# A post-norm whose factor g moves into the copy out of PSUM, and whose norm is applied on VectorE or Pool

## The chip, the cores and the metric

One core of one Trainium2 chip (trn2). Its engines are TensorE (PE in the profile), VectorE (DVE), ScalarE (ACT), Pool (GpSimd) and the DMA queues, issued by SyncE (SP). Each engine executes its own instructions in program order. The metric is the device time of one execution in microseconds.

## The reference, cut to what matters

Two layers of a streaming encoder on 1024 prompt frames and 32 sample frames, width 1024, in fp32:

```
h  = rmsnorm(x, g_pre[l])
P  = h @ w_in[l]                        # one projection, cut into three mixers
ya = gMLP(...);  yb, yc = attention of two kinds, each times silu of its gate
y  = concat(ya, yb, yc) @ w_out[l]
x  = x + rmsnorm(y, g_post[l])          # the post-norm
rmsnorm(v, g) = v * rsqrt(mean(v*v) + 1e-6) * g
```

## The kernel before

The frames lie along the free axis, in three tiles: tiles 0 and 1 of 384 columns and tile 2 of 288 (the last 32 are the sample frames). The model width lies on the partitions in eight chunks of 128. An fp32 product is taken as three products of rounded parts: the activation is split into hh and hl, the weight into whi and wlo (in rows of the profile some weights stand in buffers named kk, ph, pl or vv), and TensorE adds hh·whi, hl·whi and hh·wlo in PSUM. One block of output rows for one tile is 24 matmuls, in a PSUM tile named d or S.

A layer computes its projection blocks in the order of `ORDERS[l]`, each for all three tiles, the attention units between them, and then the eight output blocks, first all of tile 0, then of tile 1, then of tile 2. Each output block is squared for the post-norm's sum and copied out of PSUM into `Y` by ScalarE or VectorE (`copy`). Then comes `boundary(l, t)`. Ones-matmuls sum the squares over partitions, VectorE and Pool form the factor r, ident-matmuls spread it over the partitions (`rms_steps`), and ScalarE writes it to `R`. For each of the eight chunks, `x` multiplies `Y` by g and R, adds the residual chunk (buffers named s or bias) and stores the result; `x2` splits the new `Y` into hh (times the next layer's g) and hl, and adds its square, which ScalarE has written to a tmp, into a sum v. When all eight are in, the ones-matmul on v starts the norm of the next layer. The last tile of layer 1 goes through `finish` instead, where g is already applied in the copy.

The order of instructions on each engine is set when the program is built. A planner (class `Clock`) carries a modelled time for every engine and buffer; steps wait in lanes, and `look` and `pump` emit the step that the model has ready first, so that matmuls of the next blocks stand between a sum and its ones-matmul. Two helpers choose an engine by the earlier modelled end: `copy` between ScalarE and VectorE, and `two` between VectorE and Pool:

```
ends = [(clock.end(e.key, "tensor_tensor", [out], [a, b]) - bias * i, i)
        for i, e in enumerate((dve, pool))]
(dve, pool)[min(ends)[1]].tensor_tensor(out, a, b, op)
```

All engine calls pass through one recording helper, so every row of the profile carries its line, L291. Instructions are told apart by their tiles.

Of the kernel before, what the change touches and what calls it, by code (L numbers as in the profile page):

```python
# [21 lines left out]
ALU = mybir.AluOpType  # L22
# [15 lines left out]
BLOCKS = "bk bv bq0 bq1 bq2 bq3 av0 av1 ck0 ck1 cv0 cv1 cq0 cq1 au0 au1 az0 az1 bz0 bz1 bz2 bz3 cz0 cz1".split()  # L38

ORDERS = (  # L40
    "bk bv bq0 bq2 bq1 bq3 av1 cq0 cv0 ck0 av0 bz2 cq1 cv1 au0 ck1 bz1 au1 az0 az1 bz3 bz0 cz1 cz0".split(),
    "bk bv bq0 bq1 bq2 av0 ck1 cv0 bq3 bz2 bz0 av1 ck0 cq0 cq1 bz1 cv1 au1 au0 bz3 az0 az1 cz0 cz1".split(),
)

FIRST = {"b": 0, "c": 4, "a": 6}
# [261 lines left out]
def encoder(  # L307
# [87 lines left out]
    def tmp():  # L395
        return tl([128, 384], "tmp")
# [676 lines left out]

    def layer_consts(l):

        box = {}

        def mix():
            dma.dma_start(wt, aws[l])

            for g in range(4):
                pool.affine_select(wt[:, g, :], wt[:, g, :], pattern=[[1, 128]], compare_op=ALU.is_ge, fill=0.0,
                                   base=0, channel_multiplier=-1)

        def mix_bias(g):
            half = g % 2
            dma.dma_start(bsb[64 * half : 64 * half + 64, g // 2, :], abias[l, g : g + 1, :].to_broadcast([64, 128]))

        def sample_sink(j, g):
            dma.dma_start(ssk[32 * g : 32 * g + 32, j : j + 1],  # L1090
                          sinks[l : l + 1, 4 * j + g : 4 * j + g + 1].to_broadcast([32, 1]))
            if (j, g) == (1, 3):
                pool.tensor_scalar(ssk[:, 2:4], ssk[:, 0:2], -1.0, None, op0=ALU.mult)

        def table():
            c, e = box["c"], box["e"] = tmp(), tmp()
            dma.dma_start(c[:4, 0:256], crel[l, :, 1:257])
            pool.tensor_copy(c[:4, 256:384], c[:4, 255:256].to_broadcast([4, 128]))
            pool.tensor_copy(e[:4, :], c[:4, 255:256].to_broadcast([4, 384]))
            lane("store").put(lambda: dma.dma_start(fc_d[l][:, 0:384], c[:4, :]), None, lambda: after("dma", [c[:4, :]]))  # L1100
            lane("store").put(lambda: dma.dma_start(fc_d[l][:, 384:FC_W], e[:4, : FC_W - 384]), None,
                              lambda: after("dma", [e[:4, :]]), f"{l}.LC")

        return ([table, mix, lambda: dma.dma_start(gab, ag[l : l + 1, :].to_broadcast([128, 256]))]
                + [lambda g=g: mix_bias(g) for g in range(4)] + [lambda j=j, g=g: sample_sink(j, g) for j in (0, 1) for g in range(4)])

# [160 lines left out]
    def boundary(l, t, box):  # L1267

        a, T = TOK[t]
        last = l == L - 1  # L1270
        ln = lane(f"bnd{t}")
        chunk = chunks[l, t]
        rms_steps(ln, box, t, None, f"{l}.P{t}")
        nb = {}
        for k in range(8):
            y = Y[:, k, a : a + T]

            def x(k=k, y=y):
                g = g_sb[:, l, 1, k : k + 1]
                dve.scalar_tensor_tensor(y, y, g, R[:, a : a + T], op0=ALU.mult, op1=ALU.mult)  # L1280
                c = chunk.pop(k)
                two(y, y, c[:, :T], ALU.add)
                let_go(c)
                store((o_y if last else x1_d[l])[:, k, a : a + T], y)

            def x2(k=k, y=y):
                if k == 0:
                    nb["sq"] = sq_tile(t)
                h_split(l + 1, t, k)
                sq_add(nb["sq"], y, T, k == 0)  # L1290

            ln.put(x, lambda k=k: k in chunk, lambda k=k: after("dve", [R[:, a : a + T], chunk[k][:, :T]]), eng=("dve",))
            if not last:
                ln.put(x2, lambda k=k: k or free("v"), lambda y=y: after("act", [y]), f"{l + 1}.X{t}.{k}", eng=("act", "dve"))
        if not last:
            rms_steps(ln, nb, t, None, f"{l + 1}.R{t}")

    def layer_steps(l):
        units = [Unit(l, br, i, q) for br, n in (("b", 4), ("c", 2)) for i in range(n) for q in range(8 // NQ[br])]
        over = marks("0.R0") if l == 0 else marks(*(f"{l - 1}.{x}" for x in ("b3", "c1", "A", "SB", "SC")))  # L1300
        lane("lc").put(lambda: sink_consts(l), over, None, f"{l}.LS")
        for f in layer_consts(l):
            lane("lc").put(f, marks(f"{l}.b1.bias"), lambda: clock.t["dma"])
        lane("lc").put(lambda: None, None, None, f"{l}.LD")
        for i, (br, pair) in enumerate([("b", i) for i in range(4)] + [("c", i) for i in range(2)]):
            lane("bias").put(lambda br=br, pair=pair: load_bias(l, br, pair),
                             lambda br=br: f"{l}.LS" in done and (br == "b" or f"{l}.LC" in done) and "t5" in done and (l == 0 or f"{l - 1}.xl2.7" in done) and free("bias", 1 if br == "b" else 2),
                             lambda br=br: slot("bias", "dma", 1 if br == "b" else 2), f"{l}.{br}{pair}.bias")
            if (br, pair) == ("b", 1):
                sample_b_steps(l)  # L1310
        for u in units:
            u.steps()
        a_steps(l)
        sample_c_steps(l)
# [5 lines left out]
    for e, (x, t) in enumerate(plan):  # L1320
# [38 lines left out]
        if kind == "w":  # L1359
            need = [f"{l}.R{t}"]  # L1360
            if n[1] == "z" and n[0] != "a":
                need += [f"{l}.{n[0]}{n[2]}"] + ([f"{l}.S{n[0].upper()}"] if t == 2 else [])
            if n[:2] in ("au", "az"):
                need.append(f"{l}.A")

            def leave(l=l, n=n, t=t, d=d, a=a, T=T):
                evac(l, n, t, d)
                let_go(d)
                if n == ORDERS[l][-1]:
                    for k in range(KB):  # L1370
                        y = Y[:, k, a : a + T]

                        def ys(y=y, k=k):
                            split(hh[t][:, k, :], hl[t][:, k, :], y)

                        lane("ysplit").put(ys, None, lambda y=y, k=k: after("act", [y], [hh[t][:, k, :]]), f"{l}.ys{t}.{k}",
                                           eng=("act", "dve"))

            ok = marks(*need)
            lane("evac").put(leave, lambda ok=ok: ok() and free("v"), None, f"{l}.{n}.{t}")  # L1380
        else:
            if plan[e - 1][1] != t or plan[e - 1][0][0] == "w":
# [122 lines left out]
```

## Time and profile before

| what | value |
|---|---|
| device time, three runs | 1014.22, 1014.42, 1015.70 us; median 1014.42 |
| profiled execution | 1014.88 us, of which the span is 1013.2 us and 1.68 us lie around it |
| granted clock of TensorE, mean | 0.998 of 2.4 GHz |
| busy: TensorE, VectorE, ScalarE, Pool | 996.8, 762.9, 511.6, 69.5 us |
| HBM traffic | 76 GB/s over the span |

All times in the rows below are in microseconds from the start of the span, which lasts to 1013.2. The hand-over from layer 0 to layer 1 lies at about 445 to 545, the end of layer 1 from about 940 on.

### The profile page before, as it was taken

The page shows a single profiled execution, that of the slowest core. Times are in us where ns is not written, and L with a number is a line of the kernel's source. Part 1 is how long each engine was busy: PE and PEld are TensorE (multiplying, and loading weights), DVE is VectorE, ACT ScalarE, POOL GpSimd, SP SyncE. Part 2 cuts the span into 40 slices and gives each one's busy share as a digit, 9 for nine tenths or more (in the row PEclk, how much of TensorE's full clock was granted, in tenths as well). Part 3 has the DMA queues.
Part 4 walks back from the last instruction along what each step waited for, and adds up shares of the span by engine and source line. Part 5 has one row for each costly group of instructions (what it writes and reads, how often), then busy time and mean ns, then how long its engine had stood idle before and what let it go on. Part 6 is the DMA issues. An engine that isn't in the chain of part 4 may idle for free.

```text
span 1013.2 us, 18902 instructions
## 1 busy us (share of the span) xinstructions
PE 996.8 (98%) x6630; PEld 969.2 (96%) x6630; DVE 762.9 (75%) x1973; ACT 511.6 (50%) x1304; POOL 69.5 (7%) x150
## 2 busy tenths in 40 slices
PE   8999999999999999999999999999999999999997
PEld 7999999989999999999999999999899999999996
DVE  8778778877777775858897789877687787577654
ACT  7555566554444443745643566645454444356332
POOL 0100000001100000000111000000200000000121
PEclk9999999999999999999999999999999999999999
DMA  8232313212123011446543322231122212126633
GB/s 267 68 79 79 84 50 88 64 48 57 58 66 96 22 43 63 145 126 187 153 137 114 79 66 78 59 85 35 52 67 64 65 43 75 42 76 196 188 109 128
DMA packets 83343, 91.26 MB, mean 90 GB/s; under 512 B 13232, under 2 KB 59696, under 8 KB 83248
## 3 DMA queue, kind: packets, MB, share of 16 engines
q1 hardware_dynamic: 83248, 90.05, 30.2%
q8 instruction: 52, 0.85, 0.4%
q14 instruction: 43, 0.35, 0.1%
HBM read 66.11 MB, written 11.31 MB: 76 GB/s over the span
## 4 chain that ended last, share of the span: by engine, by line
PE 82%; DVE 8%; DMA 3%; ACT 3%; issue 2%; SPq 1%; POOL 1%; DVEq 0%; ACTq 0%; POOLq 0%
PE d L291 54%; PE S L291 14%; PE pt L291 8%; PE pv L291 6%; DVE Y L291 3%; DVE s L291 1%; ACT tmp L291 1%; DVE wlo L291 1%; DVE pl L291 1%; DVE v L291 1%; SPq L291 1%; DMA wraw<-in_wo_dram 1%; DVE hl L291 1%; DMA wraw<-in_w_dram 1%; DMA bias<-fb_d 1%
## 5 line engine op out<-in xcount | busy, mean ns | idle before, releaser
L291 PE MATMUL d<-hh,whi 128*128 128x384 f32 (+1 forms) x1144 | 378.6, 331 | 0.0
L291 PE MATMUL d<-hh,wlo 128*128 128x384 f32 (+1 forms) x1144 | 369.7, 323 | 0.5 <-DVE wlo L291 0.4
L291 PE MATMUL d<-hl,whi 128*128 128x384 f32 (+1 forms) x1144 | 369.0, 323 | 0.0
L291 PEld LDWEIGHTS d<-hh,whi 128*128 128x128 f32 x1144 | 215.5, 188 | 2.2 <-issue 1.7
L291 PEld LDWEIGHTS d<-hh,wlo 128*128 128x128 f32 x1144 | 215.0, 188 | 1.3 <-DVE wlo L291 1.1
L291 PEld LDWEIGHTS d<-hl,whi 128*128 128x128 f32 x1144 | 215.7, 189 | 0.3
L291 ACT ACTIVATE s<-s,nm 128x256 f32<-128x256 f32 (+5 forms) x196 | 108.5, 554 | 150.0 <-DVE nm L291 149.8
L291 DVE TENSOR_TENSOR pl<-pt,ph 128x512 fp32r<-128x512 f32 (+2 forms) x136 | 80.6, 623 | 26.2 <-ACT ph L291 25.9
L291 DVE TENSOR_TENSOR wlo<-wraw,whi 128x512 fp32r<-128x512 f32 x116 | 80.2, 693 | 14.3 <-ACT whi L291 11.0
L291 ACT ACTIVATE ph<-pt 128x512 fp32r<-128x512 f32 (+2 forms) x136 | 69.0, 542 | 25.8 <-PE pt L291 24.7
L291 DVE TENSOR_TENSOR Y<-pv,tmp 64x256 f32<-64x256 f32 x96 | 40.4, 421 | 44.2 <-ACT tmp L291 43.2
L291 PE MATMUL pv<-pl,vv 128*128 128x256 f32 (+1 forms) x288 | 71.1, 286 | 0.6 <-DVE pl L291 0.3
L291 PE MATMUL pv<-ph,vv 128*128 128x256 f32 (+1 forms) x288 | 70.0, 269 | 0.2 <-ACT ph L291 0.2
L291 PE MATMUL pt<-ident,s 128*128 128x128 f32 x488 | 68.6, 274 | 0.0
L291 ACT ACTIVATE whi<-wraw 128x512 fp32r<-128x512 f32 x94 | 58.7, 624 | 18.5 <-DMA wraw<-in_wo_dram 13.7
L291 PE MATMUL S<-kk,qh 128*128 128x256 f32 (+3 forms) x224 | 66.1, 313 | 1.2 <-DVE nm L291 1.2
L291 PE MATMUL S<-kk,ql 128*128 128x256 f32 (+3 forms) x224 | 62.1, 295 | 0.0
L291 ACT ACTIVATE tmp<-tmp 128x384 f32<-128x384 f32 (+1 forms) x48 | 23.8, 496 | 68.1 <-DVE tmp L291 68.1
L291 PEld LDWEIGHTS pt<-ident,s 128*128 128x128 f32 x488 | 56.0, 140 | 2.2 <-DVE s L291 0.5
L291 PEld LDWEIGHTS pv<-pl,vv 128*128 128x128 f32 x288 | 54.4, 189 | 3.1 <-DVE pl L291 2.4
L291 DVE CUSTOM_DVE_ANT_0 s<-S,bias,nsink 128x256 f32<-128x256 f32 (+1 forms) x128 | 54.3, 463 | 2.8 <-POOL bias L291 1.5
L291 ACT ACTIVATE tmp<-pv 64x256 f32<-64x256 f32 x96 | 36.4, 379 | 39.2 <-DVE Y L291 20.4
(183 smaller groups left out, 1765.8 us busy)
## 6 DMA issues: line engine op xcount, KB each, us to landing
wraw<-in_w_dram SPq DMA_DIRECT2D x96, 256.0 KB, 2.9
wraw<-in_wo_dram SPq DMA_DIRECT2D x72, 256.0 KB, 3.0
qr<-Y SPq DMA_DIRECT2D x384, 32.0 KB, 1.9
x_d<-Y SPq DMA_DIRECT2D x16, 192.0 KB, 3.2
out_y_dram<-Y SPq DMA_DIRECT2D x16, 192.0 KB, 2.8
Y<-in_xT_dram SPq DMA_DIRECT2D x5, 576.0 KB, 4.8
bias<-fc_d SPq DMA_DIRECT2D x8, 320.0 KB, 3.8
bias<-fb_d SPq DMA_DIRECT2D x16, 128.0 KB, 3.1
```

The costliest lines, as they stand in the source:

```text
L291: return f(*args, **kw)
```

## The change

The copy out of PSUM now multiplies every output block by its g, for all tiles of both layers. `boundary` then multiplies `Y` by `R` alone, through `two`, which takes VectorE or Pool. Two block orders change by some places, and the bias table of a layer is built in two v buffers where it was built in two tmp buffers, with its store and release by the helpers that the other stores use.

```
--- before.py
+++ after.py
@@ -38,8 +38,8 @@
 BLOCKS = "bk bv bq0 bq1 bq2 bq3 av0 av1 ck0 ck1 cv0 cv1 cq0 cq1 au0 au1 az0 az1 bz0 bz1 bz2 bz3 cz0 cz1".split()
 
 ORDERS = (
-    "bk bv bq0 bq2 bq1 bq3 av1 cq0 cv0 ck0 av0 bz2 cq1 cv1 au0 ck1 bz1 au1 az0 az1 bz3 bz0 cz1 cz0".split(),
-    "bk bv bq0 bq1 bq2 av0 ck1 cv0 bq3 bz2 bz0 av1 ck0 cq0 cq1 bz1 cv1 au1 au0 bz3 az0 az1 cz0 cz1".split(),
+    "bk bv bq0 bq2 bq1 bq3 av1 cq0 cv0 ck0 av0 bz2 cq1 cv1 au0 ck1 bz1 bz0 au1 az1 bz3 az0 cz1 cz0".split(),
+    "bk bv bq0 bq1 bq2 av0 cv0 ck1 bq3 bz2 bz0 av1 ck0 cq0 cq1 bz1 cv1 au1 au0 bz3 az0 az1 cz0 cz1".split(),
 )
 
 FIRST = {"b": 0, "c": 4, "a": 6}
@@ -1073,7 +1073,6 @@
 
     def layer_consts(l):
 
-        box = {}
 
         def mix():
             dma.dma_start(wt, aws[l])
@@ -1093,13 +1092,14 @@
                 pool.tensor_scalar(ssk[:, 2:4], ssk[:, 0:2], -1.0, None, op0=ALU.mult)
 
         def table():
-            c, e = box["c"], box["e"] = tmp(), tmp()
+            c, e = tl([128, 384], "v"), tl([128, 384], "v")
             dma.dma_start(c[:4, 0:256], crel[l, :, 1:257])
             pool.tensor_copy(c[:4, 256:384], c[:4, 255:256].to_broadcast([4, 128]))
             pool.tensor_copy(e[:4, :], c[:4, 255:256].to_broadcast([4, 384]))
-            lane("store").put(lambda: dma.dma_start(fc_d[l][:, 0:384], c[:4, :]), None, lambda: after("dma", [c[:4, :]]))
-            lane("store").put(lambda: dma.dma_start(fc_d[l][:, 384:FC_W], e[:4, : FC_W - 384]), None,
-                              lambda: after("dma", [e[:4, :]]), f"{l}.LC")
+            store(fc_d[l][:, 0:384], c[:4, :], c)
+            store(fc_d[l][:, 384:FC_W], e[:4, : FC_W - 384], e)
+            lane("store").put(lambda: None, None, None, f"{l}.LC")
+            let_go(c, e)
 
         return ([table, mix, lambda: dma.dma_start(gab, ag[l : l + 1, :].to_broadcast([128, 256]))]
                 + [lambda g=g: mix_bias(g) for g in range(4)] + [lambda j=j, g=g: sample_sink(j, g) for j in (0, 1) for g in range(4)])
@@ -1277,7 +1277,7 @@
 
             def x(k=k, y=y):
                 g = g_sb[:, l, 1, k : k + 1]
-                dve.scalar_tensor_tensor(y, y, g, R[:, a : a + T], op0=ALU.mult, op1=ALU.mult)
+                two(y, y, R[:, a : a + T], ALU.mult)
                 c = chunk.pop(k)
                 two(y, y, c[:, :T], ALU.add)
                 let_go(c)
@@ -1299,8 +1299,8 @@
         units = [Unit(l, br, i, q) for br, n in (("b", 4), ("c", 2)) for i in range(n) for q in range(8 // NQ[br])]
         over = marks("0.R0") if l == 0 else marks(*(f"{l - 1}.{x}" for x in ("b3", "c1", "A", "SB", "SC")))
         lane("lc").put(lambda: sink_consts(l), over, None, f"{l}.LS")
-        for f in layer_consts(l):
-            lane("lc").put(f, marks(f"{l}.b1.bias"), lambda: clock.t["dma"])
+        for i, f in enumerate(layer_consts(l)):
+            lane("lc").put(f, lambda i=i: f"{l}.b1.bias" in done and (i or free("v", 2)), lambda: clock.t["dma"])
         lane("lc").put(lambda: None, None, None, f"{l}.LD")
         for i, (br, pair) in enumerate([("b", i) for i in range(4)] + [("c", i) for i in range(2)]):
             lane("bias").put(lambda br=br, pair=pair: load_bias(l, br, pair),
@@ -1392,7 +1392,7 @@
                 act.activation(box["more"][:, :T], d[:, :T], AF.Square)
             else:
                 sq_add(box["sq"], d[:, :T], T, cnt == 0)
-            copy(Y[:, n, a : a + T], d[:, :T], g_sb[:, l, 1, n : n + 1] if end else None)
+            copy(Y[:, n, a : a + T], d[:, :T], g_sb[:, l, 1, n : n + 1])
             let_go(d)
             cnt += 1
             if end and cnt == KB - 1:
```

The planner then places everything anew. In what follows, names carry a buffer's number. On Pool, in the hand-over of layer 0's tile 0, from the operation that raises its r to the power (r_5798) to that of the next two; lines with a - are of before, those with a + of the change; s and bias are residual chunks:

```order
 L291 TENSOR_TENSOR r_5798<-r_5798,mhalf 128x3
-L291 TENSOR_TENSOR v_5818<-v_5818,tmp_5910 128x384
-L291 TENSOR_TENSOR r_6168<-r_6168,mhalf 128x3
-L291 TENSOR_TENSOR r_6181<-r_6181,mhalf 128x3
+L291 TENSOR_TENSOR Y<-Y,R 128x384
+L291 TENSOR_TENSOR Y<-Y,s_5465 128x384
+L291 TENSOR_TENSOR Y<-Y,R 128x384 x4
+L291 TENSOR_TENSOR Y<-Y,bias_5473 128x384
+L291 TENSOR_TENSOR Y<-Y,R 128x384 x2
+L291 TENSOR_TENSOR Y<-Y,bias_5477 128x384
+L291 TENSOR_TENSOR r_6105<-r_6105,mhalf 128x3
+L291 TENSOR_TENSOR r_6180<-r_6180,mhalf 128x3
```

Seven multiplies and three residual adds now stand on Pool where one sum v stood.

On TensorE, where the ones-matmul reads v_5840, the sum of squares of layer 1's input for tile 0 (v_5818 is the sum for layer 0's tile 1; d and S are output blocks of tiles 1 and 2). Before:

```order
L291 MATMUL S_6151<-hh_70,vv_5871 128x288
L291 MATMUL pt_6164<-ones,v_5818 128x1 x3
L291 MATMUL S_6151<-hh_70,vv_5871 128x288
L291 MATMUL S_6151<-hl_73,vv_5871 128x288
L291 MATMUL S_6151<-hh_70,vv_5871 128x288 x2
L291 MATMUL S_6151<-hl_73,vv_5871 128x288
L291 MATMUL S_6151<-hh_70,vv_5871 128x288
L291 MATMUL pt_6177<-ones,v_5840 128x1 x3
```

With the change:

```order
L291 MATMUL d_6087<-hh_69,vv_5875 128x384
L291 MATMUL d_6087<-hl_72,vv_5875 128x384
L291 MATMUL d_6087<-hh_69,vv_5875 128x384 x2
L291 MATMUL d_6087<-hl_72,vv_5875 128x384
L291 MATMUL d_6087<-hh_69,vv_5875 128x384 x2
L291 MATMUL d_6087<-hl_72,vv_5875 128x384
L291 MATMUL d_6087<-hh_69,vv_5875 128x384
L291 MATMUL pt_6101<-ones,v_5840 128x1 x3
L291 MATMUL d_6087<-hh_69,vv_5875 128x384
```

The ones-matmul on v_5840 has moved ahead of the one on v_5818, from behind 18 of the 24 matmuls of tile 2's first block to behind 9 of 24 matmuls of tile 1's fifth. Between it and the ident-matmul on r_5798 stood 168 matmuls of 128x384 and 18 of 128x288; now 129 of 128x384 stand there.

On TensorE, where the next hand-over ends. v_6195 is the sum for layer 0's tile 2 in both; the sum of layer 1's input for tile 1 is v_6220 before and v_6229 now; d_6497 is the last output block, d_6535, d_6543 and S_6604 are blocks of layer 1. Before:

```order
L291 MATMUL d_6535<-hh_68,wlo_6504 128x384
L291 MATMUL pt_6569<-ones,v_6195 128x1 x3
L291 MATMUL d_6535<-hh_68,whi_6503 128x384
L291 MATMUL d_6535<-hl_71,whi_6503 128x384
L291 MATMUL d_6535<-hh_68,wlo_6504 128x384
L291 MATMUL d_6535<-hh_68,whi_6503 128x384
L291 MATMUL d_6535<-hl_71,whi_6503 128x384
L291 MATMUL d_6535<-hh_68,wlo_6504 128x384
L291 MATMUL d_6535<-hh_68,whi_6503 128x384
L291 MATMUL d_6535<-hl_71,whi_6503 128x384
L291 MATMUL d_6535<-hh_68,wlo_6504 128x384
L291 MATMUL pt_6595<-ones,v_6220 128x1 x3
```

With the change:

```order
L291 MATMUL d_6497<-hh_70,wlo_6440 128x288
L291 MATMUL d_6543<-hh_68,whi_6469 128x384
L291 MATMUL d_6543<-hl_71,whi_6469 128x384
L291 MATMUL d_6543<-hh_68,wlo_6470 128x384
L291 MATMUL pt_6551<-ones,v_6229 128x1 x3
L291 MATMUL d_6543<-hh_68,whi_6469 128x384
L291 MATMUL d_6543<-hl_71,whi_6469 128x384
L291 MATMUL d_6543<-hh_68,wlo_6470 128x384
L291 MATMUL pt_6565<-ones,v_6195 128x1 x3
```

The ones-matmul for tile 1's sum now stands three matmuls into layer 1's first block and ahead of the one on v_6195; before it stood behind that block's 24, and behind the other.

## Rows read from the trace of the kernel before

**Rows 1.** The page: busy time of each engine over the span with the number of instructions, then the chain that ended last.

```profile
PE 996.8 (98%) x6630; PEld 969.2 (96%) x6630; DVE 762.9 (75%) x1973; ACT 511.6 (50%) x1304; POOL 69.5 (7%) x150
...
PE 82%; DVE 8%; DMA 3%; ACT 3%; issue 2%; SPq 1%; POOL 1%; DVEq 0%; ACTq 0%; POOLq 0%
```

**Rows 2.** Busy time of each engine in three stretches of the hand-over from layer 0 to layer 1, one for each tile (stretch, its length, then busy time and number of instructions of PE, PEld, DVE, ACT and POOL, the granted clock of TensorE, the share and GB/s of the DMA engines).

```profile
449.50:480.90 31.40, 31.40 (x188) 31.40 (x187) 26.77 (x48) 18.76 (x41) 1.01 (x1) 1.00 0.57 176
484.00:510.00 26.00, 25.76 (x190) 25.43 (x190) 24.09 (x42) 18.09 (x41) 4.34 (x4) 1.00 0.59 174
514.00:540.00 26.00, 25.05 (x154) 24.54 (x154) 22.09 (x56) 10.15 (x29) 3.02 (x12) 1.00 0.40 125
```

**Rows 3.** The timeline of TensorE around the hand-over of tiles 0 and 1: start, duration (us), engine, line, operation, tiles, size, how many in a row.

```profile
467.71 0.34 PE L291 MATMUL d<-hh,ph 128*128 128x384 f32 x1
...
469.80 0.34 PE L291 MATMUL d<-hh,vv 128*128 128x384 f32 x1
...
473.95 0.34 PE L291 MATMUL S<-hh,vv 128*128 128x384 f32 x1
...
481.18 0.72 PE L291 MATMUL pt<-ones,v 128*128 128x1 f32 x6
...
482.63 0.83 PE L291 MATMUL pt<-ident,r 128*128 128x128 f32 x6
483.21 0.38 PE L291 MATMUL d<-hh,vv 128*128 128x288 f32 x1
```

**Rows 4.** The timeline of VectorE from the first norm on (same columns, with idle time before it and what ended it).

```profile
449.56 0.62 DVE L291 SCALAR_TENSOR_TENSOR Y<-Y,g_sb,R 128x384 f32<-128x384 f32 x1 [3.23 <-ACT R L291]
...
456.50 0.61 DVE L291 SCALAR_TENSOR_TENSOR hl<-Y,g_sb,hh 128x384 fp32r<-128x384 f32 x1
457.03 0.55 DVE L291 TENSOR_TENSOR v<-v,tmp 128x384 f32<-128x384 f32 x1
457.50 0.61 DVE L291 SCALAR_TENSOR_TENSOR Y<-Y,g_sb,R 128x384 f32<-128x384 f32 x1
...
459.43 0.68 DVE L291 TENSOR_TENSOR vv<-wraw,vv 128x512 fp32r<-128x512 f32 x1
460.03 0.68 DVE L291 TENSOR_TENSOR pl<-wraw,ph 128x512 fp32r<-128x512 f32 x1
...
484.02 0.62 DVE L291 SCALAR_TENSOR_TENSOR Y<-Y,g_sb,R 128x384 f32<-128x384 f32 x1 [1.93 <-ACT R L291]
```

**Rows 5.** TensorE's timeline at the waits of the hand-over's end, with the matmuls that give the pitches, and the late one near the end.

```profile
505.84 0.30 PE L291 MATMUL d<-hh,wlo 128*128 128x288 f32 x1
...
506.37 0.34 PE L291 MATMUL d<-hh,whi 128*128 128x384 f32 x1
...
509.42 0.83 PE L291 MATMUL pt<-ones,v 128*128 128x1 f32 x6 [0.24 <-POOL v L291]
...
512.73 0.80 PE L291 MATMUL pt<-ones,v 128*128 128x1 f32 x6 [0.79 <-DVE r L291]
...
536.29 0.55 PE L291 MATMUL pt<-ident,v 128*128 128x128 f32 x3 [0.91 <-DVE v L291]
536.60 0.42 PE L291 MATMUL d<-hh,ph 128*128 128x384 f32 x1
...
990.99 0.41 PE L291 MATMUL S<-hh,wlo 128*128 128x288 f32 x1 [0.80 <-DVE wlo L291]
```

**Rows 6.** The timeline where Pool and VectorE work side by side: in each pair the operation of Pool and the one of VectorE beside it.

```profile
458.07 1.01 POOL L291 TENSOR_TENSOR v<-v,tmp 128x384 f32<-128x384 f32 x1 [10.78 <-ACT tmp L291]
458.14 1.36 DVE L291 TENSOR_TENSOR Y<-Y,s 128x384 f32<-128x384 f32 x1
...
501.00 1.03 POOL L291 TENSOR_TENSOR v<-v,tmp 128x288 f32<-128x288 f32 x1 [1.33 <-ACT tmp L291]
501.29 1.17 DVE L291 SCALAR_TENSOR_TENSOR Y<-Y,g_sb,R 128x384 f32<-128x384 f32 x1
...
984.12 0.81 POOL L291 TENSOR_TENSOR v<-v,tmp 128x288 f32<-128x288 f32 x1 [0.30 <-ACT tmp L291]
984.15 1.19 DVE L291 SCALAR_TENSOR_TENSOR Y<-Y,g_sb,R 128x384 f32<-128x384 f32 x1
```

**Rows 7.** Groups of instructions over the whole span, different shapes apart: line, engine, operation, tiles, size, how many | busy us, mean ns | idle before.

```profile
L291 DVE SCALAR_TENSOR_TENSOR Y<-Y,g_sb,R 128x384 f32<-128x384 f32 x32 | 23.6, 739 | 11.5 <-ACT R L291 11.5
...
L291 ACT ACTIVATE Y<-d,g_sb 128x288 f32<-128x288 f32 x5 | 2.5, 496 | 0.0
...
L291 ACT ACTIVATE Y<-d 128x288 f32<-128x288 f32 x5 | 2.0, 404 | 0.0
```

**Rows 8.** VectorE's timeline in the hand-over of tile 2.

```profile
520.07 0.51 DVE L291 SCALAR_TENSOR_TENSOR hl<-Y,g_sb,hh 128x288 fp32r<-128x288 f32 x1
520.50 0.45 DVE L291 TENSOR_TENSOR v<-v,tmp 128x288 f32<-128x288 f32 x1
520.86 0.51 DVE L291 SCALAR_TENSOR_TENSOR Y<-Y,g_sb,R 128x288 f32<-128x288 f32 x1
```

**Rows 9.** Busy time and granted clock (PEclk) in three stretches of the start (columns as in rows 2).

```profile
10.00:12.00 2.00, 1.15 (x6) 0.52 (x4) 1.90 (x5) 2.00 (x5) 0.00 (x0) 1.00 0.73 260
12.00:14.00 2.00, 1.64 (x6) 1.65 (x7) 2.00 (x5) 2.00 (x5) 0.00 (x0) 0.66 0.98 301
14.00:16.00 2.00, 2.00 (x8) 2.00 (x7) 2.00 (x4) 1.87 (x5) 0.00 (x0) 0.50 0.83 252
```

More of the change, by code (lines that the diff above doesn't have):

```diff
@@ L40 @@
 ORDERS = (
-    "bk bv bq0 bq2 bq1 bq3 av1 cq0 cv0 ck0 av0 bz2 cq1 cv1 au0 ck1 bz1 au1 az0 az1 bz3 bz0 cz1 cz0".split(),
-    "bk bv bq0 bq1 bq2 av0 ck1 cv0 bq3 bz2 bz0 av1 ck0 cq0 cq1 bz1 cv1 au1 au0 bz3 az0 az1 cz0 cz1".split(),
+    "bk bv bq0 bq2 bq1 bq3 av1 cq0 cv0 ck0 av0 bz2 cq1 cv1 au0 ck1 bz1 bz0 au1 az1 bz3 az0 cz1 cz0".split(),
+    "bk bv bq0 bq1 bq2 av0 cv0 ck1 bq3 bz2 bz0 av1 ck0 cq0 cq1 bz1 cv1 au1 au0 bz3 az0 az1 cz0 cz1".split(),
 )
@@ L1074, in layer_consts @@
     def layer_consts(l):
-        box = {}
         def mix():
@@ L1095, in table @@
         def table():
-            c, e = box["c"], box["e"] = tmp(), tmp()
+            c, e = tl([128, 384], "v"), tl([128, 384], "v")
             dma.dma_start(c[:4, 0:256], crel[l, :, 1:257])
@@ L1099, in table @@
             pool.tensor_copy(e[:4, :], c[:4, 255:256].to_broadcast([4, 384]))
-            lane("store").put(lambda: dma.dma_start(fc_d[l][:, 0:384], c[:4, :]), None, lambda: after("dma", [c[:4, :]]))
-            lane("store").put(lambda: dma.dma_start(fc_d[l][:, 384:FC_W], e[:4, : FC_W - 384]), None,
-                              lambda: after("dma", [e[:4, :]]), f"{l}.LC")
+            store(fc_d[l][:, 0:384], c[:4, :], c)
+            store(fc_d[l][:, 384:FC_W], e[:4, : FC_W - 384], e)
+            lane("store").put(lambda: None, None, None, f"{l}.LC")
+            let_go(c, e)
         return ([table, mix, lambda: dma.dma_start(gab, ag[l : l + 1, :].to_broadcast([128, 256]))]
@@ L1279, in x @@
                 g = g_sb[:, l, 1, k : k + 1]
-                dve.scalar_tensor_tensor(y, y, g, R[:, a : a + T], op0=ALU.mult, op1=ALU.mult)
+                two(y, y, R[:, a : a + T], ALU.mult)
                 c = chunk.pop(k)
@@ L1301, in layer_steps @@
         lane("lc").put(lambda: sink_consts(l), over, None, f"{l}.LS")
-        for f in layer_consts(l):
-            lane("lc").put(f, marks(f"{l}.b1.bias"), lambda: clock.t["dma"])
+        for i, f in enumerate(layer_consts(l)):
+            lane("lc").put(f, lambda i=i: f"{l}.b1.bias" in done and (i or free("v", 2)), lambda: clock.t["dma"])
         lane("lc").put(lambda: None, None, None, f"{l}.LD")
@@ L1394, in encoder @@
                 sq_add(box["sq"], d[:, :T], T, cnt == 0)
-            copy(Y[:, n, a : a + T], d[:, :T], g_sb[:, l, 1, n : n + 1] if end else None)
+            copy(Y[:, n, a : a + T], d[:, :T], g_sb[:, l, 1, n : n + 1])
             let_go(d)
```

## The prediction

> **What bounds the kernel now.** I read the page first, for the engine that never rests. TensorE is busy 98% of the span and carries 82% of the chain that ended last [rows 1], so the time moves only where TensorE stands still or runs at its lower clock. VectorE is busy 75%, but that is a mean. In the stretches where layer 0 hands over to layer 1 it is nearly full: 26.77 of 31.40 us for tile 0, 24.09 of 26.00 for tile 1, 22.09 of 26.00 for tile 2 [rows 2]. There lies the change: `boundary` multiplies, adds the residual, splits into hh and hl and sums squares, and a ones-matmul on TensorE waits for the last sum.
>
> TensorE executes in program order, so the place of that ones-matmul decides who waits. For tile 0 the norm reaches VectorE at 449.56 [rows 4], and TensorE takes the sum at 481.18 with no idle time shown before it [rows 3]. At the end of the next hand-over two ones-matmuls came 0.24 and 0.79 us late, and a later ident-matmul 0.91 [rows 5]: 1.94 us, most of what TensorE loses in this part.
>
> **What one multiply costs where.** The fused multiply Y·g·R takes 0.61 us when alone and has a pitch of 0.64 (457.50 to 458.14) [rows 4, 6]; hl has one of 0.53, an add or a sum 0.47, a 128x512 subtraction 0.60 [rows 4]; for tile 2, 0.43 for hl and 0.36 for a sum [rows 8]. Pool's two-operand operation of 128x384 takes 1.01 us, of 128x288 0.81 [rows 6]. What matters more: while Pool runs one, a VectorE operation that reads two operands from SBUF is held. The 128x384 add at 458.14 took 1.36 beside Pool, and a sum of that size 0.55 alone; fused multiplies took 1.17 and 1.19 beside Pool's 128x288, against 0.61 [rows 4, 6]. So a Pool operation costs a full VectorE about 0.8 us (128x384) or 0.6 (128x288): more than the 0.47 of a plain multiply on VectorE itself.
>
> The Trainium skill (GPSIMD Engine Reference, Specifications) says that Pool's SBUF interfaces are shared with VectorE, with contention for VectorE instructions that have two SBUF inputs. These rows agree; by that rule no multiply sent to Pool is free while VectorE has such work.
>
> **The change part by part.**
>
> Copies out of PSUM: ScalarE's copy with g takes 496 ns against 404 without (128x288) [rows 7], 0.09 more each, on an engine busy 18.76 of 31.40 us [rows 2]. Zero; ScalarE's idle time hides it. Uncovered it would be 0.09 us for each of eight copies of a tile, 0.7.
>
> Removed: 40 fused multiplies on VectorE, 32 of them of 128x384 [rows 7]. By the order, 13 come back there as a plain multiply and 27 go to Pool: 7, 5 and 5 for the tiles of layer 0, 5 and 5 in layer 1. Residual adds and sums move too: in the three hand-overs Pool now executes 10, 9 and 9 operations, where before it had 1, 4 and none.
>
> Moved: TensorE asks for the sums sooner. I count operations in the order and take matmul pitches of 0.174 us for 128x384 (12 from 467.71 to 469.80) and 0.1325 for 128x288 (four from 505.84 to 506.37) [rows 3, 5].
>
> Tile 0: the ident-matmul that starts it stands in the same row in both programs. The ones-matmul of 481.18 now stands 15 matmuls ahead of the S block that began at 473.95: 473.95 - 15 × 0.174 = 471.3. From 449.56 VectorE has 21.8 us, not 31.6. Ahead of the last sum its order has 35 operations: 17 multiplies, adds and sums (17 × 0.47 = 8.0), 10 hl and hh (10 × 0.53 = 5.3), 8 of 128x512 (4.8): 18.1 us. Pool's 10 hold it for 10 × 0.8 = 8.0. I take 0.2 for the signal to TensorE, an estimate near the 0.24 of rows 5. 26.3 - 21.8 = **4.5 us** of new wait. From below: if all of Pool's work falls into VectorE's idle time, 18.3, no wait. From above: 4.6 us of the old stretch were idle on VectorE [rows 2]; 3 of them coming back would give 7.5. I stay with the sum, since idle time both lengthens VectorE's stretch and gives Pool free room.
>
> Tile 1: from ident-matmul 482.63 to the next matmul 0.58, to the first multiply 1.39 [rows 3, 4]. Then 165 matmuls of 128x288 and 3 of 128x384: 0.58 + 21.9 + 0.5 - 1.39 = 21.6 us. VectorE's 38 operations: 16 × 0.47 + 4 × 0.37 + 9 × 0.53 + 9 × 0.60 = 19.2. Pool: 7 × 0.8 + 2 × 0.6 = 6.8. 26.2 - 21.6 = **4.6 us**; bounds 0 and 6.
>
> Tile 2: 108 matmuls of 128x384 (18.8), 8 score matmuls at no more than a 128x288 (1.1), two ident groups at 0.31 (0.6) [rows 5], 0.58 - 1.39: 19.7 us. VectorE: 9 × 0.43, 14 × 0.37, and 14 operations of layer 1's keys, values and queries at about a sum's 0.47: 15.7. Pool 9 × 0.6 = 5.4. 21.3 - 19.7 = **1.6 us**; bounds 0 and 3.
>
> Layer 1's boundaries ask for no sum of squares. What waits there is one matmul at 990.99, 0.80 behind VectorE's wlo, just after Pool and VectorE held each other around 984.12 [rows 5, 6]. Five multiplies gone to Pool: 5 × (0.8 - 0.64); three that stay save 0.17 each: +0.3. I take **+0.5**, bounds -0.8 and +1.5.
>
> Gained back: 0.24, 0.79 and 0.91 [rows 5]. The first two end in the earlier places; ahead of the third, VectorE's order now has the value that TensorE needs before the scores that stood in its way: **-1.9**.
>
> At nothing: the block orders (the same matmuls, TensorE has others beside them) and the bias table in v buffers, written well before its use. If that cover went, the price is a wait as at 536.29, 0.9 us [rows 5].
>
> Sum: 4.5 + 4.6 + 1.6 + 0.5 - 1.9 = +9.3. The profiled execution took 1014.88 (span 1013.2 and 1.68 around it), 0.46 over the median of 1014.42; so 1024.2 in its terms, **1023.7** beside the median.
>
> **The rivals.**
>
> Faster: the multiplies fit. Pool is busy 7% [rows 1], and VectorE has idle time in each stretch. If Pool's work falls there, the new waits are zero, -1.9 stays and 990.99 gives back 0.8: 1014.42 - 2.7 = 1011.7. It decides if Pool's ten operations hold VectorE under 0.35 us each (21.8 - 0.2 - 18.1 = 3.5). Against: each hold of rows 6 is 0.56 or more. For: the one Pool sum in the old first stretch cost TensorE nothing. 19%.
>
> About the same: holds of 0.5 us. Then the waits are 1.5, 2.3 and 0.7; less 1.9 and up to 1 elsewhere: +1.6, 1016.0. For: the old stretch with four Pool sums lost TensorE about 1.0 us at its two ones-matmuls [rows 5]. 13%.
>
> Slower, with the clock on top. In 10 to 12 us TensorE was busy 1.15 of 2 us, and then its granted clock was 0.66 and 0.50 of 2.4 GHz, the lower level of 1.2 GHz in the last [rows 9]: 2 × 0.34 + 2 × 0.50 = 1.7 us lost. Two long waits could each cost that: 1023.7 + 3.4 = 1027.1. 8%. The Trainium skill (TensorE: Matmul & The Clock Gate, HAM oscillation) has idle gaps of TensorE taking the clock back to its lower level; the start of this trace agrees, and whether waits like these bring it about in the middle no row tells.
>
> **How the numbers follow.** My forecast, waits at the first two hand-overs and a small third, 60%. With holds of 0.56, the smallest, and no wait at tile 2 or in layer 1: 2.1 + 2.8 - 1.9 = +3.0, 1017; with the upper ends, 7.5 + 6 + 1.6 + 1.5 - 1.9 = +14.7, 1029. That is its own range. For 8 in 10 I take 1011 to 1030: down to the faster rival and up past the clock's, leaving out the clock on top of the longest waits. A measurement of this kernel tells about 0.2%, 2 us, from no change: faster 0.19, same 0.13, slower 0.68.
>
> **What would show it.** Idle time of some 4 us on TensorE before the ones-matmul for tile 0 near 471, and as much before that for tile 1, ended by VectorE's v; Pool's Y<-Y,R at 1.0 us or more, with adds and hl of VectorE at 1.1 to 1.4 beside them; VectorE near 100% busy there. If there is no gap near 471, or VectorE keeps 0.55 beside Pool, the step of the holds is wrong, and the time is 1011 to 1013. If the gap is there and the total is not, TensorE got back elsewhere what I count as fixed.

## The result

The changed kernel takes 1030.32 us (median of 4 runs, 1029.22 to 1031.04) against 1015.06 for the kernel before, timed beside it: a ratio of 1.0142 with a 95% interval of 1.0129 to 1.0156, slower by about 14.4 us (the medians lie 15.3 apart). The profiled execution took 1030.6 us, its span 1028.9, which is 15.7 more than before.

### The profile page after: what moved, and what is told of

Its sections match the earlier page's. It is cut to its first block, busy times and chain, and to the rows that moved or that the text cites. A ratio compares the mean times of both kernels' runs of the same rounds, so it can differ in the third digit from the quotient of the medians.

```text
span 1028.9 us, 18896 instructions
## 1 busy us (share of the span) xinstructions
PE 1001.5 (97%) x6630; PEld 972.5 (95%) x6630; DVE 763.8 (74%) x1935; ACT 513.1 (50%) x1304; POOL 113.2 (11%) x188
## 4 chain that ended last, share of the span: by engine, by line
PE 77%; DVE 12%; ACT 3%; issue 3%; DMA 3%; SPq 2%; POOL 0%; DVEq 0%; ACTq 0%; POOLq 0%
PE d L291 51%; PE S L291 13%; PE pt L291 8%; PE pv L291 6%; DVE Y L291 3%; SPq L291 2%; DVE v L291 2%; DVE s L291 1%; ACT tmp L291 1%; DVE pl L291 1%; DVE hl L291 1%; DVE wlo L291 1%; DMA wraw<-in_wo_dram 1%; ACT s L291 1%; DMA bias<-fb_d 1%
## 5 line engine op out<-in xcount | busy, mean ns | idle before, releaser
L291 ACT ACTIVATE ph<-pt 128x512 fp32r<-128x512 f32 (+2 forms) x136 | 68.8, 540 | 26.6 <-PE pt L291 25.8
L291 ACT ACTIVATE whi<-wraw 128x512 fp32r<-128x512 f32 x91 | 56.6, 624 | 13.5 <-DMA wraw<-in_wo_dram 8.4
L291 DVE TENSOR_TENSOR v<-v,tmp 128x384 f32<-128x384 f32 (+1 forms) x76 | 44.0, 582 | 25.5 <-ACT tmp L291 24.3
```

Of the source, the lines that this page charges most:

```text
L291: return f(*args, **kw)
```

## The profile after

The page of the changed kernel, busy times and the chain that ended last; they answer to [rows 1]:

```profile
PE 1001.5 (97%) x6630; PEld 972.5 (95%) x6630; DVE 763.8 (74%) x1935; ACT 513.1 (50%) x1304; POOL 113.2 (11%) x188
...
PE 77%; DVE 12%; ACT 3%; issue 3%; DMA 3%; SPq 2%; POOL 0%; DVEq 0%; ACTq 0%; POOLq 0%
```

VectorE lost 38 operations and is no less busy: what it saved came back as longer operations beside Pool. Its share of the chain grew from 8 to 12%. TensorE's waits in the hand-over, from its timeline; they answer to [rows 3, 5]:

```profile
475.13 0.80 PE L291 MATMUL pt<-ones,v 128*128 128x1 f32 x6 [3.95 <-DVE v L291]
...
512.76 0.40 PE L291 MATMUL d<-hh,wlo 128*128 128x288 f32 x1 [1.60 <-DVE wlo L291]
...
516.89 1.16 PE L291 MATMUL pt<-ones,v 128*128 128x1 f32 x6 [1.99 <-DVE v L291]
...
546.11 0.33 PE L291 MATMUL S<-kk,ql 128*128 128x128 f32 x1 [1.56 <-DVE ql L291]
...
553.63 0.85 PE L291 MATMUL pt<-ident,r 128*128 128x128 f32 x6 [0.94 <-POOL r L291]
```

Those are tile 0 (3.95), tile 1 (1.60 and 1.99) and tile 2 (1.56 and 0.94), 10.0 us; the waits of 0.24, 0.79 and 0.91 in [rows 5] are gone. VectorE's timeline in tile 0's stretch, and a row of Pool's beside it; they answer to [rows 4, 6]:

```profile
449.81 1.25 DVE L291 TENSOR_TENSOR Y<-Y,s 128x384 f32<-128x384 f32 x1
451.17 0.98 DVE L291 TENSOR_SCALAR hh<-Y,g_sb 128x384 fp32r<-128x384 f32 x1
452.19 1.26 DVE L291 SCALAR_TENSOR_TENSOR hl<-Y,g_sb,hh 128x384 fp32r<-128x384 f32 x1
...
455.76 1.37 DVE L291 TENSOR_TENSOR v<-v,tmp 128x384 f32<-128x384 f32 x1
...
463.10 0.61 DVE L291 SCALAR_TENSOR_TENSOR hl<-Y,g_sb,hh 128x384 fp32r<-128x384 f32 x1
463.63 0.54 DVE L291 TENSOR_TENSOR v<-v,tmp 128x384 f32<-128x384 f32 x1
...
451.90 4.82 POOL L291 TENSOR_TENSOR Y<-Y,R 128x384 f32<-128x384 f32 x4
```

And the same stretch in two windows, with Pool busy and without (columns as in [rows 2]):

```profile
449.30:462.10 12.80, 12.80 (x75) 12.80 (x74) 12.59 (x11) 6.19 (x13) 12.49 (x10) 1.00 0.31 93
463.10:475.00 11.90, 8.09 (x47) 7.76 (x45) 11.90 (x25) 10.51 (x22) 0.00 (x0) 1.00 0.79 240
```

While Pool executes its ten operations, VectorE gets through 12 in 13.9 us (449.22 to 463.10), about one to each of Pool's; then 25 in 11.9. Both windows show VectorE full, so it has no idle time into which Pool could fall. Last, the clock. The same view for two longer stretches and a piece of each; the granted clock is the third figure from the end:

```profile
470.00:486.00 16.00, 12.05 (x67) 11.76 (x66) 7.09 (x15) 7.25 (x16) 0.86 (x1) 0.89 0.50 163
500.00:530.00 30.00, 26.14 (x159) 25.39 (x158) 23.54 (x41) 15.70 (x34) 8.31 (x9) 0.89 0.61 184
...
476.00:478.00 2.00, 2.00 (x8) 2.00 (x8) 0.13 (x2) 0.00 (x0) 0.86 (x1) 0.55 0.99 344
...
518.00:520.00 2.00, 2.00 (x10) 2.00 (x9) 0.85 (x2) 0.98 (x2) 0.86 (x1) 0.50 0.87 288
```

After the waits at tile 0 and at tile 1 the clock granted to TensorE fell to 0.50 of 2.4 GHz, its lower level of 1.2 GHz. In the waits themselves it was still 1.00 (471 to 475 and 513 to 517), so the loss falls on work. Full-speed work lost: 16 × 0.11 = 1.8 and 30 × 0.11 = 3.3 us, 5.1 in all. After the waits at tile 2 it stayed at 1.00.

So the 15.7 us are: waits of 10.3 (the five above and one of 0.27 at 507.70) less the old 1.9, 8.4; the clock 5.1; and a remainder of 2.2, lost in layer 1's attention between about 555 and 605 us, where the planner placed things differently and no single wait stands out. That last piece was not taken apart.

## The experiments

Each is compared with the kernel before on the same chip.

**e1: the same order, the 27 multiplies on VectorE.** `two` asks the planner as before, and where it says Pool, the multiply is booked on Pool and executed by VectorE.

```
+        if i and on_dve[0]:
+            clock.run("pool", "tensor_tensor", [out], [a, b])
+            nc.vector.tensor_tensor(out, a, b, op)
```

> The changed kernel with its planner and its orders untouched; only the 27 multiplies Y<-Y,R that the planner gave to Pool are executed by VectorE, at the same places of the program. Theory (a Pool operation holds VectorE about 0.8 us, a plain multiply costs it 0.47): VectorE gains 0.33 us for each, so the wait before tile 0's ones-matmul falls from 3.95 us to about 1.6 to 2.2, that of tile 1 by some 1.6, and if the shorter waits leave the clock up, 5 us more come back: 1020 to 1025 us. Rival (holds cost nothing, the sums are simply asked too early): seven more multiplies on VectorE at 0.47 lengthen the wait at tile 0 to 7 us and the time to 1033 or more.

Measured: 1035.85 us, ratio 1.0199 (1.0183 to 1.0216). Slower still, in the rival's range, but not for the rival's reason: the wait at tile 0 was 4.82 us, neither its 7 nor the theory's 1.6 to 2.2. VectorE's timeline in tile 0's stretch:

```profile
453.85 0.43 DVE L291 TENSOR_SCALAR hh<-Y,g_sb 128x384 fp32r<-128x384 f32 x1 [1.12 <-POOL Y L291]
...
468.65 0.62 DVE L291 SCALAR_TENSOR_TENSOR hl<-Y,g_sb,hh 128x384 fp32r<-128x384 f32 x1 [1.55 <-ACT hh L291]
...
475.47 0.62 DVE L291 SCALAR_TENSOR_TENSOR hl<-Y,g_sb,hh 128x384 fp32r<-128x384 f32 x1 [1.53 <-ACT hh L291]
...
466.57 1.39 POOL L291 TENSOR_TENSOR Y<-Y,bias 128x384 f32<-128x384 f32 x1 [12.76 <-DVE Y L411]
```

VectorE has 4.2 us of idle time that it did not have in the changed kernel. The residual add of three chunks was still Pool's; its multiply now came from VectorE late and in order, and the result went to Pool, to ScalarE's hh and back to VectorE's hl, with nothing queued that could fill the gap. So this run changed two things and says little about the price of a hold. The next was made for that.

**e5: the residual adds of these chunks on VectorE as well.** Same order; all that `boundary` gives to Pool is executed by VectorE.

```
                 on_dve[0] = True
                 two(y, y, R[:, a : a + T], ALU.mult)
                 c = chunk.pop(k)
                 two(y, y, c[:, :T], ALU.add)
                 on_dve[0] = False
```

> As the run with the multiplies on VectorE in the changed kernel's order, and now the residual adds that the planner gave to Pool as well, so that no result of a hand-over travels from VectorE to Pool and on to ScalarE's hh. Theory (a hold of 0.76 us is dearer than 0.47 on VectorE; the run before lost to three such trips, with VectorE idle 1.12, 1.55 and 1.53 us): tile 0 waits 18.1 + 10 x 0.47 + 0.2 - 21.8 = 1.2 us instead of 3.95, tile 1 about 2.3, tile 2 none: 1018.5 us if the clock stays up, 1023.5 if it falls all the same. Rival (Pool's holds are no dearer than the work on VectorE; the early places of the ones-matmuls are all): waits as long as in the changed kernel, 1030 or more.

Measured: 1030.94 us, ratio 1.0159 (1.0146 to 1.0172), as slow as the changed kernel, which is the rival's time. The wait at tile 0 did shorten, and the clock took it back:

```profile
472.07 1.20 PE L291 MATMUL pt<-ones,v 128*128 128x1 f32 x5 [2.56 <-DVE v L291]
...
470.00:475.00 5.00, 2.93 (x11) 2.96 (x12) 3.16 (x7) 2.40 (x5) 0.86 (x1) 0.70 0.60 176
475.00:478.00 3.00, 3.00 (x12) 3.00 (x12) 0.00 (x0) 0.00 (x0) 0.00 (x0) 0.50 0.15 51
478.00:480.00 2.00, 2.00 (x12) 2.00 (x12) 0.00 (x0) 1.00 (x3) 0.00 (x0) 0.79 0.00 0
```

2.56 us in place of 3.95, but 5 × 0.30 + 3 × 0.50 + 2 × 0.21 = 3.4 us lost to the clock there in place of 1.8. Two things follow. The ones-matmul stands too early for VectorE even when Pool does nothing, and the holds make it worse by 1.4 us at tile 0, half of what was expected: VectorE's stretch took 24.3 us (447.55 to 471.86), not 22.8. Of these 1.5 us, 0.9 come of eight adds that stand right behind the multiply that they read: they start 0.58 behind it, not 0.47.

**e2: TensorE kept busy while it waits.** Transposes of the identity stand before the two ones-matmuls; the planner does not know of them.

```
+FILL = {"1.R0": 36, "1.R1": 18}
+        for _ in range(fill):
+            nc.tensor.transpose(s[:, 0:128], ident, ident)
```

> The changed kernel with 36 extra 128x128 transposes of the identity on TensorE right before tile 0's ones-matmul (layer 1's norm) and 18 before tile 1's, into the PSUM tile that the ones-matmuls then overwrite; the planner does not know of them. They fill the waits of 3.95 and 1.99 us at about 0.11 us each and do nothing useful. Theory (after these waits TensorE's clock fell to 0.5 and that costs 1.7 us at the first and 3.4 at the second): the granted clock stays at 1.0 after the first, and the time falls by 1.7 to 5.1 us, to 1025 to 1028.6. Rival (the clock's fall does not come of the idle wait, or costs nothing that the later waits don't absorb): 1030, or slower where the transposes overshoot the waits.

Measured: 1028.92 us, ratio 1.0136 (1.012 to 1.0151), just outside the expected 1025 to 1028.6. Five stretches:

```profile
472.00:476.00 4.00, 4.00 (x37) 3.85 (x35) 3.96 (x9) 3.01 (x7) 0.00 (x0) 1.00 0.97 337
476.00:478.00 2.00, 2.00 (x14) 2.00 (x14) 0.00 (x0) 0.00 (x0) 0.86 (x1) 1.00 0.98 348
...
516.00:518.00 2.00, 2.00 (x15) 2.00 (x14) 0.66 (x2) 0.86 (x2) 0.84 (x1) 1.00 0.96 311
...
542.00:544.00 2.00, 1.90 (x8) 1.73 (x8) 1.69 (x4) 0.80 (x3) 0.00 (x0) 0.50 0.40 131
...
546.00:548.00 2.00, 2.00 (x8) 2.00 (x8) 0.94 (x6) 1.80 (x8) 0.57 (x4) 0.50 0.54 138
```

With the idle time filled the clock stays at 1.00 after both waits, and TensorE reaches the second group of ident-matmuls behind them at 519.58 instead of 524.76. It had led by 0.2 before tile 0's wait: 5.0 us gained, close to the 5.1 counted above as the price of the clock. Then a third wait, for the first scores, brought the clock down where the changed kernel had kept it, and most was lost again.

**e9: the third wait filled too.**

```
+                for _ in range(24 if <layer 1's first scores> else 0):
+                    nc.tensor.transpose(bank[:, 0:128], ident, ident)
```

> The changed kernel with the 36 and 18 idle transposes of the second run, and 24 more right before layer 1's first score matmul, where TensorE waited 0.71 and 1.08 us for qh and ql and the clock then fell to 0.5 from 541 to 550 us. Theory (the clock's fall after waits costs time of its own): the granted clock is 1.00 through the hand-over, and the 5.0 us by which the second run led until 540 us stay: 1024.5 to 1026. Rival (what one wait gives back the next takes): 1028 to 1030 as in the second run.

Measured: 1025.84 us, ratio 1.0101 (1.0087 to 1.0115). The granted clock is 1.00 through the hand-over:

```profile
468.00:484.00 16.00, 16.00 (x115) 15.81 (x114) 7.95 (x16) 8.00 (x17) 0.86 (x1) 1.00 0.55 177
484.00:500.00 16.00, 16.00 (x123) 16.00 (x123) 12.44 (x17) 9.09 (x20) 8.77 (x9) 1.00 0.30 93
500.00:516.00 16.00, 14.27 (x106) 13.58 (x106) 15.30 (x28) 10.62 (x23) 3.72 (x4) 1.00 0.74 227
516.00:532.00 16.00, 16.00 (x99) 15.96 (x98) 12.99 (x21) 5.93 (x13) 9.54 (x11) 1.00 0.33 105
532.00:548.00 16.00, 15.31 (x103) 14.70 (x101) 12.22 (x38) 7.01 (x22) 1.85 (x9) 1.00 0.40 106
```

Doing useless work in the waits makes the kernel some 4 us faster than the changed one. What remains, 11 us over before, is the waits themselves and the piece in layer 1's attention.

**e11: e5 with the three waits filled.** The edits of e5 and e9 together, with 24 transposes at each place.

> The fifth run (the changed kernel's order, multiplies and residual adds of the hand-over on VectorE) with 24 idle transposes at each of the same three waits. There the waits were 2.56 us at tile 0 against the changed kernel's 3.95, but the clock stayed low for longer, which hid it. Theory (a hold costs more than the operation on VectorE, and the clock only hid that): with the clock up in both, this one is 1.5 to 4 us faster than the run with three waits filled: 1021 to 1023.5. Rival (Pool's holds cost no more than VectorE's own work): equal to it within 1 us.

Measured: 1022.7 us, ratio 1.0072 (1.0058 to 1.0086): 3.1 us faster than e9, timed side by side with it. The clock is at full speed here too; the two stretches of e11 in which the waits of tiles 0 and 1 lie:

```profile
468.00:484.00 16.00, 16.00 (x111) 15.88 (x109) 8.30 (x17) 7.16 (x15) 0.85 (x1) 1.00 0.46 140
...
500.00:516.00 16.00, 15.34 (x116) 14.87 (x116) 15.20 (x30) 11.01 (x24) 2.77 (x3) 1.00 0.78 223
```

So 3.1 us is what Pool's 27 multiplies and the adds beside them cost over the same work on VectorE, in this order. It is a part of the loss, not most of it: 7.8 us over before are left with that work on VectorE and the clock up.

**e8: the sums asked for later.** Pool keeps all that it has; the planner is told that three sums come later.

```
+LATE = {"1.R0": 5000.0, "1.R1": 5000.0, "1.R2": 3000.0}
-        ln.put(one, ok, lambda: max(... slot("pt", "pe")), pe=True)
+        ln.put(one, ok, lambda: max(... slot("pt", "pe")) + LATE.get(mark, 0.0), pe=True)
```

> The changed kernel, whose planner is told that the three sums of squares for layer 1's norm come 5, 5 and 3 us later than it reckons, so that it puts the ones-matmuls later among the other matmuls (tile 0's by 18 of them, tile 1's behind tile 2's post-norm) and places what follows anew. Pool keeps its multiplies. Theory (the wait is the ones-matmuls' early place against held sums): waits at the hand-over of 0 to 3 us in all and no fall of the clock at tile 0: 1014 to 1021. Rival (VectorE and Pool together are too slow whatever the place): the waits move to the next reader and the time stays at 1027 or more.

Measured: 1017.75 us, ratio 1.0029 (1.0017 to 1.004): 11 to 12 us of the loss are gone with Pool's multiplies still there. TensorE's ones-matmul for tile 0, and what is left at tile 1:

```profile
474.11 0.72 PE L293 MATMUL pt<-ones,v 128*128 128x1 f32 x6
...
505.21 0.41 PE L293 MATMUL d<-hh,wlo 128*128 128x288 f32 x1 [1.70 <-DVE wlo L293]
...
509.71 0.80 PE L293 MATMUL pt<-ones,v 128*128 128x1 f32 x6 [1.31 <-DVE v L293]
```

At tile 0 TensorE does other matmuls first and waits for nothing. Behind the two waits at tile 1 the clock fell here too (0.50 from 512 to 514), which is part of the 3 us that remain.

**e7: the old order, with Pool's multiplies.** The kernel before, its order kept by telling the planner nothing; the chunks that the change gives to Pool are multiplied there, g is in the copies.

```
+                clock.run("dve", "scalar_tensor_tensor", [y], [y, g, R[:, a : a + T]])
+                (nc.gpsimd if ON_POOL[l, t][k] == "P" else nc.vector).tensor_tensor(y, y, R[:, a : a + T], ALU.mult)
```

> As the run with the old order, but 27 of the 40 multiplies are executed by Pool: the same chunks that the change gives to it (7, 5, 5, 5, 5), at the old places of the program. Theory (the loss needs both: Pool's holds, and ones-matmuls that ask sooner): per multiply a hold of 0.76 takes the place of 0.64, some 0.8 us for tile 0, which idle time of VectorE covers; waits of 1 to 2 us in all: 1015 to 1018. Rival (multiplies on Pool are dear by themselves): 1022 or more.

Measured: 1017.37 us, ratio 1.0025 (1.0015 to 1.0035). Seven multiplies on Pool in tile 0's hand-over, and the ones-matmul on its sum, which waits for nothing:

```profile
448.44 2.68 POOL L1291 TENSOR_TENSOR Y<-Y,R 128x384 f32<-128x384 f32 x2 [2.30 <-ACT R L293]
457.88 6.83 POOL L1291 TENSOR_TENSOR Y<-Y,R 128x384 f32<-128x384 f32 x5
...
480.01 0.74 PE L293 MATMUL pt<-ones,v 128*128 128x1 f32 x6
```

Together with e8 this shows the cause from both sides: a kernel with Pool's multiplies in places that leave time for them takes about 3 us more than before, in the change's places 15. Pool's own share is much the same in either order: e7 takes 2.9 us more than e6 below, which differs from it only in the engine of these multiplies, and e9 took 3.1 more than e11. The rest of the 15 came of the places (7.8 in e11) and of the clock that the waits there brought down (4 to 5).

**e4: the block orders alone**, in the kernel before.

> The kernel before with the two block orders of the change and nothing else. Theory (orders only place the same matmuls elsewhere): 1013 to 1016.5. Rival (the new orders bring part of the loss by themselves): 1017 or more.

Measured: 1015.68 us, ratio 1.0008 (0.9997 to 1.0019): no difference that can be told.

**e3: the multiply always on VectorE, and planned so.**

```
-                two(y, y, R[:, a : a + T], ALU.mult)
+                dve.tensor_tensor(y, y, R[:, a : a + T], ALU.mult)
```

> The changed kernel with the multiply by R always on VectorE, as a plain two-operand operation, and the planner told so: it places everything anew. Block orders, bias table and g in the copies as in the change. Theory (Pool's multiplies are the loss): no wait over 1 us before the ones-matmuls, and 40 multiplies at 0.47 in place of 0.64 leave VectorE 6.8 us less to do: 1011.5 to 1014. Rival (the block orders or g in the copies do the harm): 1020 or more.

Measured: 1022.16 us, ratio 1.0063 (1.0043 to 1.0082). The time is the rival's, but neither account fits. In the hand-over all went as the theory had it: the waits before ones-matmuls are 0.44 and 0.81 us, and at 590 us this kernel leads the one before by 2.7, of which it already led 1.5 at 430. It loses 11 later, in layer 1's attention, where it waits for weights. Two of TensorE's waits, and SyncE's queue:

```profile
606.36 0.44 PE L291 MATMUL d<-hh,whi 128*128 128x384 f32 x1 [0.99 <-ACT whi L291]
627.35 0.45 PE L291 MATMUL d<-hh,whi 128*128 128x384 f32 x1 [1.87 <-ACT whi L291]
...
592.19 0.52 SPq L291 DMA_DIRECT2D wraw<-in_w_dram  x1
593.16 13.12 SPq L291 DMA_DIRECT2D qr<-Y  x16
606.39 1.00 SPq L291 DMA_DIRECT2D bias<-fb_d  x2
607.49 1.87 SPq L291 DMA_DIRECT2D wraw<-in_w_dram  x2
```

In the order planned anew, 16 transfers of queries stand on SyncE between two loads of weights and hold the queue for 13 us; the next weights come late, and again at 627 and 648. The three waits make 4.7 us, and the clock fell behind the last two (0.79 over 626 to 634, 0.81 over 647 to 656), 3.4 us more; the other 3 were not taken apart. That block orders and g in the copies, which the rival blamed, are not the reason is shown by e4 and e6. A small edit replans everything behind it. This is why the other runs keep an order fixed wherever they can.

**e6, e10, e12: the old order with ever less on Pool.** e6 is e7 with all 40 multiplies on VectorE. e10 also executes the sums of squares there that the planner gives to Pool, at the same places. e12 does the same for every other operation that `two` gives to Pool.

```
+        if i and here:                 # e12: if i:
+            clock.run("pool", "tensor_tensor", [out], [a, b])
+            nc.vector.tensor_tensor(out, a, b, op)
```

> The kernel before with its own order on all engines, instruction for instruction; only g is multiplied in by the copies out of PSUM, and the fused multiply of a hand-over is a plain Y times R on VectorE. Theory: VectorE saves 0.17 us at each of 40 multiplies, which takes up to 1.0 us from the waits of 0.24 and 0.79 us and up to 0.8 from that near the end: 1012.5 to 1014.5, in the measurement's noise or just below before. Rival (copies with g make ScalarE late): 1016 or more.

> As the run with the old order and plain multiplies on VectorE, and the sums of squares that the planner gives to Pool (one of 128x384 and four of 128x288 in the hand-over, four in layer 1) are executed by VectorE at the same places. Theory (a hold is dearer than the operation): VectorE saves some 0.2 us at each, about 1 us ahead of the ones-matmuls that still come 0.36 and 0.94 us late: 1013 to 1014.5, at the limit of what can be told. Rival (VectorE is the bound there and Pool relieves it): 1015.5 or more.

> As the run with the sums on VectorE, and every other two-operand operation that the planner chose to give to Pool (four hl, the splits wlo, pl and vv of weights, ql, in all layers) executed by VectorE at its place; Pool keeps the powers, the memsets and the two fixed adds of the last tile. Theory (a Pool operation of 128x512 takes 1.3 to 1.4 us and holds VectorE, which needs 0.60 for it): no slower than the run before, 1011.5 to 1013. Rival (outside the hand-over VectorE has work of its own on the path, and Pool relieves it): 1013.5 or more.

Measured: e6 1014.52 us, ratio 1.0002 (0.9993 to 1.0011); e10 1012.63 us, 0.9977 (0.9966 to 0.9987); e12 1014.25 us, 0.9999 (0.9989 to 1.0008). In e6 the 0.17 us saved at each of 40 multiplies bought nothing that can be told. e10 is the one kernel here that beats both the kernel before and the changed one. Its two ones-matmuls at the end of the hand-over, where before showed 0.24 and 0.79 [rows 5]:

```profile
508.82 0.80 PE L291 MATMUL pt<-ones,v 128*128 128x1 f32 x6 [0.16 <-DVE v L409]
...
511.13 0.72 PE L291 MATMUL pt<-ones,v 128*128 128x1 f32 x6
```

Near the end the wait of 0.80 [rows 5] is gone as well. So even the few sums that Pool had in the kernel before were better left to VectorE. e12 went too far: its expectation, no slower than e10, was wrong by 1.6 us. In its trace a ones-matmul waits 0.59 us again at 508.53, and a matmul at 995.22 waits 0.94 for VectorE's ph; that the splits of weights and queries, now VectorE's, stood in the way is argued and not shown.

## Why the prediction was right, and where it was short

The direction and the mechanism held; 1030.3 lies just outside the range of 1011 to 1030, while the paired ratio on the median shown (1014.42 × 1.0142 = 1028.8) lies inside.

- **Tile 0, 4.5 us:** 3.95. VectorE's stretch to the last sum was worked out at 18.1 + 8.0 = 26.1 us and took 25.8 (449.22 to 474.98), without a gap. A hold cost 0.74 us: 12 operations took 13.9 us beside ten of Pool's; the same twelve take 6.5 in e5, where Pool is idle. Pool's operations did not fall into idle time; there was none.
- **Tile 1, 4.6:** 0.27 + 1.60 + 1.99 = 3.9. Part of it came as a late weight, since VectorE's wlo beside Pool took 1.48 us.
- **Tile 2, 1.6:** 1.56 + 0.94 = 2.5, at other readers than forecast: the first scores (VectorE's ql queued behind boundary work) and a late r of Pool.
- **Gained back, 1.9:** as worked out. **Layer 1, +0.5:** nothing. The wait near its end fell from 0.80 to 0.35, but TensorE lost the 0.45 again in the next 6 us: against the same matmuls of before it was 15.67 us behind at 990.29 and 15.69 at 1023.78.
- **The clock, put aside as a rival at 8% with 3.4 us:** 5.1 us, and it came again in e1 and e5, whose waits were idle too. This is the term that was mis-sized: what the rows at the start showed (1.7 us) should have stood in the sum, since the forecast itself had two waits of over 4 us. It was also left out of the upper end: 1029 took no clock, and tile 2 at 1.6 where its stated bound was 3; that bound alone gives 1030.5.
- **The sentence that a hold is dearer than the multiply it saves** was right, but its weight was overrated. e5 and e11 put it at 1.4 us for tile 0 and 3.1 in all. What decides is the place: the planner asked for tile 0's sum 9.9 us sooner, and VectorE cannot have it by then with or without Pool. Why the planner took it to be ready stays open. Its model does charge for the sharing (`Clock.end` starts an operation behind one of the other engine that it has already placed), and no run took that model apart.

The faster rival fell with VectorE's full windows, which left Pool's work no room; "about the same" fell with holds of 0.74.

## What to carry to other kernels

When a planner moves elementwise work to a second engine and then asks for its results sooner, check the first engine's total in that stretch against the new due time, with the price of the holds in it: that sum, from a trace of the old kernel, was right to 0.3 us of 26. A wait on TensorE costs its length and can cost a spell of half speed behind it, here 1.8 and 3.3 us; give both a place in the sum. To tell a change from the replanning that it sets off, keep the order of instructions fixed and change only the engine that executes them.

## What the runs showed of the hardware beyond that

- VectorE's hh, which reads one tensor from SBUF and writes SBUF, was held by Pool too: 0.98 us at 451.17 against 0.42 when alone (e5's 448.81). The prediction expected holds only for operations that read two operands from SBUF. The Trainium skill (GPSIMD Engine Reference, Specifications) names VectorE instructions in a 2-port performance mode beside those with two SBUF inputs; whether hh runs in such a mode no row tells.
- The fall of the clock did not grow with the wait. After 3.95 us of idle time it cost 1.8 us, after 2.56 us (e5) 3.4, and with the idle time filled by useless transposes nothing. The Trainium skill (TensorE: Matmul & The Clock Gate, HAM oscillation) has idle gaps bring the clock down; these runs agree for the waits of the first two hand-overs, and add that a busy TensorE keeps it though nothing useful is done.
- The wait alone does not decide. A wait of 1.79 us at 521.34 in e7 left the clock at 1.00, as did those of 1.56 and 0.94 at tile 2 in the changed kernel, while 1.70 and 1.31 in e8 brought it down. And one and the same wait at the start, in the kernel before and in e8, was followed by 0.66 and 0.50 in before [rows 9] and by 1.00 in e8:

```profile
12.36 0.46 PE L291 MATMUL S<-hl,whi 128*128 128x384 f32 x1 [1.04 <-DVE hl L291]
...
12.17 0.44 PE L293 MATMUL S<-hl,whi 128*128 128x384 f32 x1 [1.04 <-DVE hl L293]
...
12.00:14.00 2.00, 1.83 (x10) 1.73 (x11) 2.00 (x5) 2.00 (x5) 0.00 (x0) 1.00 1.00 313
```

The first line is of before, the other two of e8. A single profiled execution is thus no price list for the clock.
